# One power on GpSimd for the inverse root of the norms, and the kept first block in place of a rebuilt one

## The chip, the cores and the metric

The kernel runs on one core of a Trainium2 chip. The metric is the device time of one execution in microseconds (us), the median of three runs.

A core has a matrix engine (TensorE, PE in the profile, with PEld for its weight loads), a vector engine (VectorE, DVE), a scalar engine (ScalarE, ACT), a general engine (GpSimd, POOL), and a queue engine (SyncE, SP). Each works through its own list of instructions in order, and waits for the others through semaphores.

## The reference

Two layers of a decoder trunk, on 2048 positions of width 1024: first a gated matrix memory (mLSTM), then a gated linear recurrence (RG-LRU), each behind an RMS norm with a residual sum, and a last RMS norm. The part that the change touches is the norm, and the projection behind it:

```python
def rmsnorm(x, g):
    xf = x.astype(jnp.float32)
    y = xf * lax.rsqrt(jnp.mean(xf * xf, axis=-1, keepdims=True) + EPS)
    return (y * g.astype(jnp.float32)).astype(x.dtype)
...
    for layer in range(DEPTH):
        u = rmsnorm(x, ln_g[layer])
        if layer % N_MIXERS == 0:
            y = mlstm_mixer(u, ...)      # proj = u @ w_in, then convolution, gates, memory, w_out
        else:
            y = rglru_mixer(u, ...)      # proj = u @ w_in, then convolution, gates, scan, w_out
        x = x + y
    return rmsnorm(x, final_g)
```

## The kernel before, in words

The activations are held transposed: a tile has 128 of the 1024 features on its partitions and 512 positions (one block) along it. There are four blocks. Every float32 product is done as three matmuls of rounded parts: a number is split into `hi` and `lo` (`split_into`, lines 735 to 738: ACT makes `hi`, DVE subtracts it to make `lo`), and `mm3` (lines 362 to 364) adds hi*hi, hi*lo and lo*hi.

The phases follow one another: `phase_a1` (first norm and first projection, up to about 1000 us), `phase_a2` (the matrix memory, to about 1710 us), `phase_b1` (output projection of layer one, second norm and second projection, to about 2560 us), `phase_b2` (gates, scan, output projection, last norm).

**Slabs.** The two projections use a scheme of seven products in place of eight (Winograd's form of Strassen's) on a *slab* of two blocks. A slab `s` consists of a first block and a second one. The first block gives `u`, its normed value, in eight tiles `xs`, split into the operands `u11` (features 0 to 511) and `u21` (512 to 1023). The second block `x1` is scaled to its own `u`, and both are combined into the operands `t1` to `t4` and `u22`. `combos` (line 196) does this on DVE: it scales eight tiles (line 207) with the rows of the inverse root, and makes the sums and differences and their splits, some 44 DVE steps for a slab. While DVE does so, the PE has only products of the first block to work on: `early` (line 230) runs 6 weight groups with `u11` and `u21` alone, and calls hooks between them: `stat` (line 607) and `norm` (line 610). `stat` makes the inverse root of the second block's norm (`invrms`) and calls `backs` (line 187), which rebuilds the first block's `u` from its parts, eight DVE additions `hi + lo` (line 185) into the tiles `t1h` and `t4l`. `norm` calls `combos`. `group` (line 249) then runs the remaining five products of each weight group. The second projection (`phase_b1`) uses the same helpers.

**Norms.** `stats_sum` (line 1019) adds the squares over the partitions with 4 small matmuls (`ssum`, line 1024), forms mean + eps on DVE (`stx`, line 1027: 128 x 4 numbers), and calls `rsqrt` (line 334). This starts from the shifted bit pattern (lines 338 and 339) and makes three Newton rounds of three steps (lines 341 to 343): eleven DVE steps on 128 x 4 numbers, each needing the one before. The result `rc` is spread over the partitions by the matmuls `rows` (line 140) or `srow` (line 1034). There are twelve such norms: four blocks for each of three RMS norms.

**Weights.** Raw weights come by SP's queue into eight `raw` buffers, are combined on DVE (`sum`, line 117), split into eight slots `s`, and the splits of combined weights are stored by POOL's queue (`d_wx`, `d_wr`; line 90) for the second slab.

**Order.** The program hands the instructions to a planner, which orders them for each engine by priority and by the time at which it reckons them ready; weight preparation has high priority. So the order on an engine is not the order of the program text, and the order of one engine can put a step behind another that waits.

The matrix memory (`phase_a2`) already has a power on POOL, for its own norm of two numbers a partition (line 967).

Of the kernel before, what the change touches and what calls it, by code (L numbers as in the profile page):

```python
# [7 lines left out]
F32 = mybir.dt.float32  # L8
F32R = mybir.dt.float32r
I32 = mybir.dt.int32  # L10
AF = mybir.ActivationFunctionType
ALU = mybir.AluOpType
PSUM = bass.MemoryType.PSUM

P = 128
T = 2048
DM = 1024
KD = DM // P
# [8 lines left out]
EPS = 1e-6  # L27
# [11 lines left out]
class Slab:  # L39
# [153 lines left out]
            self.back(f2[j], U, "u21", j, self.nc.vector)  # L193
        return f1, f2

    def combos(self, U, xs, rc, fs, row=None):

        f1, f2 = fs
        v = self.nc.vector
        pb = self.rows(rc)  # L200
        if row is not None:
            self.nc.scalar.copy(row, pb)
            pb = row
        us = xs if row is not None else [self.x() for _ in range(KD)]
        for j in range(4):
            for k in (j, j + 4):
                v.scalar_tensor_tensor(us[k], xs[k], self.K.v(self.gain, k), pb, op0=ALU.mult, op1=ALU.mult)
            x12, x22 = us[j], us[j + 4]
            t = self.temp("t4", "h", j)
            v.tensor_tensor(t, x22, x12, op=ALU.subtract)  # L210
            U["t3", j] = self.operand("t3", j, t, "v")
            v.tensor_tensor(x12, x12, f1[j], op=ALU.subtract)
            v.tensor_tensor(f1[j], f1[j], t, op=ALU.add)
            U["t2", j] = self.operand("t2", j, f1[j], "v")
        for j in range(4):
            U["u22", j] = self.operand("u22", j, us[j + 4], "v")
            v.tensor_tensor(us[j + 4], f2[j], f1[j], op=ALU.subtract)
        for j in range(4):
            U["t1", j] = self.operand("t1", j, us[j], "v")
        for j in range(4):  # L220
            U["t4", j] = self.operand("t4", j, us[j + 4], "v")
# [67 lines left out]
class Trunk:  # L289
    def __init__(self, ctx, tc, vecs, gbias):  # L290
        self.tc = tc
        self.nc = nc = tc.nc
        cp = ctx.enter_context(tc.tile_pool(name="const", bufs=1))
        self.cp = cp
        self.tail = []
        self.vec = cp.tile([P, NVEC], F32, name="vec")
        nc.sync.dma_start(self.vec, vecs)
        self.gb = cp.tile([64, 2], F32, name="gb")
        nc.sync.dma_start(self.gb, gbias)
        self.ident = cp.tile([P, P], F32, name="ident")  # L300
        make_identity(nc, self.ident)
        self.ones = cp.tile([P, 1], F32, name="ones")
        nc.vector.memset(self.ones, 1.0)
        self.one1 = cp.tile([1, 1], F32, name="one1")
        nc.vector.memset(self.one1, 1.0)
        self.lc = cp.tile([P, 48], F32, name="lc")
        self.gT = cp.tile([P, 64], F32, name="gT")
        self.wlT = cp.tile([P, 64], F32, name="wlT")
        self.enT = cp.tile([P, 64], F32, name="enT")
        self.dl = cp.tile([P, 64], F32, name="dl")  # L310
# [20 lines left out]
        o = VOFF[name] + i  # L331
        return self.vec[:, o:o + 1]

    def rsqrt(self, pool, out, x, w, rows=P):
        nc = self.nc
        b = pool.tile([P, w], I32, tag="rsb", name="rsb")
        t = pool.tile([P, w], F32, tag="rst", name="rst")
        nc.vector.tensor_scalar(b[:rows], x.bitcast(I32), 1, None, op0=ALU.logical_shift_right)
        nc.vector.tensor_scalar(out.bitcast(I32), b[:rows], -1.0, float(0x5F3759DF), op0=ALU.mult, op1=ALU.add)
        for _ in range(3):  # L340
            nc.vector.tensor_tensor(t[:rows], out, out, op=ALU.mult)
            nc.vector.scalar_tensor_tensor(t[:rows], t[:rows], -0.5, x, op0=ALU.mult, op1=ALU.mult)
            nc.vector.scalar_tensor_tensor(out, t[:rows], 1.5, out, op0=ALU.add, op1=ALU.mult)

    def stats(self, pool, psp, acc, rc, rb, tag="st"):

        nc = self.nc
        ps = psp.tile([P, 512], F32, tag=tag, name=tag)
        for c in range(4):
            nc.tensor.matmul(ps[:, c:c + 1], acc[:, c * P:(c + 1) * P], self.ones, start=True, stop=True)  # L350
        x = pool.tile([P, 4], F32, tag="stx", name="stx")
        nc.vector.tensor_scalar(x, ps[:, 0:4], 1.0 / DM, EPS, op0=ALU.mult, op1=ALU.add)
        self.rsqrt(pool, rc, x, 4)
        pb = psp.tile([P, 512], F32, tag=tag, name=tag)
        for c in range(4):
            nc.tensor.matmul(pb[:, c * P:(c + 1) * P], rc[:, c:c + 1].to_broadcast([P, P]), self.ident,
                             start=True, stop=True)
        nc.scalar.copy(rb, pb)

    def mm3(self, out, sh, sl, mh, ml, first, last, resumed=False):  # L360
        mm = self.nc.tensor.matmul
# [23 lines left out]
    def phase_a1(self, xT, woq, wxz, D):  # L385
        tc, nc = self.tc, self.nc
        with ExitStack() as ctx:
            S = Slab(self, ctx, "g0")
# [93 lines left out]
            def load(b):  # L482

                xs = fetch([S.x() for _ in range(KD)], b)
                return xs, squares(xs)

            def ahead(b):
                return fetch(S.ahead(), b)
# [103 lines left out]
            with tc.high_priority():  # L592
                xs, acc = load(0)
                prefetch(1)
                x1 = ahead(1)
                acc1 = squares(x1, True)
            pb = S.rows(S.invrms(acc))
            U = {}
# [5 lines left out]
            for s in range(2):  # L604
                t = []

                def stat():
                    t[:] = [S.invrms(acc1), S.backs(U)]

                def norm():  # L610
                    S.combos(U, x1, *t)
                p1 = S.early(NE, lambda j: ew[j] if j < 2 * s else stream(1, s), U, lambda j: out_of(first[j], s),
                             ([] if s else [None, None]) + [stat, norm])
                for j, i in enumerate(first):
                    S.group(stream(), U, out_of(i, s), p1=p1[j])
                gates = iter(())
                for j, (kind, i) in enumerate(middle):
                    W = stream()
                    if kind == "q":
                        o_group(W, i, s, U)  # L620
                        if i == H - 1 and s == 1:
                            gates = self.gates(wk, pm, G, D)
                        continue
                    if s == 0 and j == 1:
                        lt = wk("lam")
                        parts = iter(range(8))

                        def lpart(r, w):
                            i = next(parts) * 64
                            return lt[0:r, i:i + w]  # L630
                        self.decay_rates(lpart)
                    next(gates, None)
                    if s == 0 and j == 5:
                        xs, acc = load(2)
                    if s or j < len(middle) - 1:
                        n2 = {}
                        if s == 0 and j == len(middle) - 3:
                            rc = []
                            n2 = {"t2": lambda: rc.append(S.invrms(acc)), "t1": lambda: S.scale(xs, rc[0])}
                        S.group(W, U, out_of(i, s), n2)  # L640
                        continue
                    V, n1 = {}, []
                    with tc.high_priority():
                        er = [S.raws(wxz[i], ("11", "12")) for i in first[0:2]]

                    def after_t2():
                        S.parts(V, xs[0:4], "u11", "v")
                        n1.extend(ahead(3))

                    def after_u21():  # L650
                        for e, r in enumerate(er):
                            ew.append({nm: S.operand("t3", e * 2 + q, r[nm], "v") for q, nm in enumerate(r)})
                        S.parts(V, xs[4:8], "u21", "v")
                    S.group(W, U, out_of(i, s), {"t2": after_t2, "u21": after_u21, "t4": lambda: n1.append(squares(n1, True))})
                    U = V
                    x1, acc1 = n1[0:KD], n1[KD]
# [362 lines left out]
    def stats_sum(self, pool, psp, sums, rc, tag):  # L1019
        nc = self.nc  # L1020
        ps = psp.tile([P, 512], F32, tag=tag, name="ssum")
        for c in range(4):
            for i, a in enumerate(sums):
                nc.tensor.matmul(ps[:, c:c + 1], a[:, c * P:(c + 1) * P], self.ones, start=i == 0,
                                 stop=i == len(sums) - 1)
        x = pool.tile([P, 4], F32, tag="stx", name="stx")
        nc.vector.tensor_scalar(x, ps[:, 0:4], 1.0 / DM, EPS, op0=ALU.mult, op1=ALU.add)
        self.rsqrt(pool, rc, x, 4)

    def stats_rows(self, psp, rc, tag):  # L1030
        nc = self.nc
# [466 lines left out]
```

## Time and profile before

| | us |
|---|---|
| median of three runs | 3058.34 (3058.22 to 3059.42) |
| profiled execution | 3061.18 |
| its span in the profile | 3059.1 |
| PE busy in the span | 2927.9 |
| DVE busy | 2153.6 |
| ACT busy | 1509.3 |
| POOL busy | 211.7 |

The granted clock of the PE over the span is 0.983 of full speed.

How to read the profile lines below. A line of a group names the source line, the engine, the operation, the tiles (out<-in), shapes and the count; behind the bar stand the busy time in us, the mean of one in ns, and the idle time of that engine just before. A line of the timeline begins with the start and the duration in us, and ends with the idle time before it and what ended that, in brackets. A line of waits has the total in us, the number of times, and the longest. A line of the windows has a stretch, its length, and the busy time of PE, PEld, DVE, ACT and POOL with the number of instructions, then the granted clock, the share of the DMA engines, and GB/s. Times count from the start of the span.

### The profile page before, as it was taken

How to read it: one execution, taken by the hardware profiler on the slowest of the kernel's cores; microseconds unless marked ns; L12 is line 12 of the kernel's file. 1: busy time of each engine (PE TensorE's matmuls, PEld its weight loads, DVE VectorE, ACT ScalarE, POOL GpSimd, SP SyncE). 2: the span in 40 equal slices, each digit the busy share in tenths (PEclk: the TensorE clock that was granted, in tenths of full speed). 3: DMA queues.
4: the chain of work that ended last, by engine and by line, in shares of the span. 5: the costliest groups of instructions: out<-in, count | busy, mean ns of one | idle time of the engine just before them, and what ended most of it. 6: DMA issues, size and time to landing. Idle time of an engine off the chain costs nothing. (4 is left out here: it accounts for less than half of the span.)

```text
span 3059.1 us, 43718 instructions
## 1 busy us (share of the span) xinstructions
PE 2927.9 (96%) x15730; PEld 2506.7 (82%) x15730; DVE 2153.6 (70%) x3774; ACT 1509.3 (49%) x2514; POOL 211.7 (7%) x394
## 2 busy tenths in 40 slices
PE   6999999999999999999999899999999998899997
PEld 4799987899988898989999777877888886687786
DVE  7866789534566688888888555687778374887775
ACT  5444545323344566666666322333445234876772
POOL 0111110000000011111111000000110000110100
PEclk9999999999999999999999999999999998999999
DMA  6766677666777645454443665566666656656643
GB/s 218 255 216 231 230 249 241 204 202 206 222 222 228 193 129 167 128 171 132 148 144 102 200 192 176 182 210 216 217 216 224 206 188 230 240 183 236 237 134 128
DMA packets 308985, 600.63 MB, mean 196 GB/s; under 512 B 27808, under 2 KB 106400, under 8 KB 308768
## 3 DMA queue, kind: packets, MB, share of 16 engines
q1 hardware_dynamic: 222784, 389.79, 41.4%
q10 hardware_dynamic: 59184, 107.77, 10.0%
q0 software_dynamic: 26800, 100.28, 8.5%
q8 instruction: 124, 2.03, 0.3%
q14 instruction: 93, 0.76, 0.1%
HBM read 388.86 MB, written 208.86 MB: 195 GB/s over the span
## 5 line engine op out<-in xcount | busy, mean ns | idle before, releaser
L735 ACT CAST s<-raw 128x512 fp32r<-128x512 f32 (+1 forms) x360 | 222.3, 621 | 497.8 <-PE acc L364 195.4
L738 DVE TENSOR_TENSOR s<-raw,s 128x512 fp32r<-128x512 f32 (+1 forms) x360 | 246.9, 689 | 90.4 <-ACT s L735 84.9
L362 PE MATMUL acc<-yh,s 128*128 128x512 f32 x512 | 202.3, 398 | 10.1 <-ACT yh L735 3.4
L363 PE MATMUL acc<-yl,s 128*128 128x512 f32 x512 | 202.8, 396 | 0.0
L364 PE MATMUL acc<-yh,s 128*128 128x512 f32 x512 | 202.2, 395 | 0.0
L362 PE MATMUL acc<-yh,wh 128*128 128x512 f32 x384 | 150.4, 399 | 14.3 <-ACT yh L735 9.4
L363 PE MATMUL acc<-yl,wh 128*128 128x512 f32 x384 | 153.5, 401 | 0.3 <-DVE yl L738 0.2
L364 PE MATMUL acc<-yh,wl 128*128 128x512 f32 x384 | 152.1, 399 | 1.1 <-DVE wl L738 1.0
L662 DVE SCALAR_TENSOR_TENSOR xc<-xm,vec,xc 128x512 f32<-128x512 f32 x192 | 140.5, 748 | 14.3 <-ACT xc L660 13.4
L735 ACT CAST s<-sum 128x512 fp32r<-128x512 f32 (+1 forms) x120 | 74.3, 620 | 146.4 <-PE pa L364 43.6
L362 PEld LDWEIGHTS acc<-yh,s 128*128 128x128 f32 x512 | 96.6, 189 | 35.5 <-ACT yh L735 3.8
L735 ACT CAST wh<-wr 128x512 fp32r<-128x512 f32 (+1 forms) x104 | 65.4, 641 | 107.8 <-PE acc L363 76.1
L364 PEld LDWEIGHTS acc<-yh,s 128*128 128x128 f32 x512 | 96.8, 189 | 22.7
L363 PEld LDWEIGHTS acc<-yl,s 128*128 128x128 f32 x512 | 96.8, 189 | 22.4 <-DVE yl L738 0.4
L930 DVE SCALAR_TENSOR_TENSOR C<-C,dl,kv 128x516 f32<-128x516 f32 x112 | 83.7, 747 | 44.6 <-PE kv L364 44.5
L738 DVE TENSOR_TENSOR wl<-wr,wh 128x512 fp32r<-128x512 f32 (+1 forms) x104 | 73.5, 717 | 56.2 <-ACT wh L735 50.9
L362 PE MATMUL gate<-xch,wh 128*128 128x512 f32 x224 | 91.9, 411 | 19.2 <-ACT xch L735 9.3
L738 DVE TENSOR_TENSOR s<-sum,s 128x512 fp32r<-128x512 f32 (+1 forms) x120 | 82.6, 689 | 39.3 <-ACT s L735 38.0
L662 DVE SCALAR_TENSOR_TENSOR xc<-xr,vec,xc 128x512 f32<-128x512 f32 x144 | 104.9, 747 | 7.3 <-ACT xc L660 6.3
L735 ACT CAST Ch<-C 128x516 fp32r<-128x516 f32 x120 | 74.8, 623 | 64.9 <-DVE da L948 48.2
L362 PE MATMUL pj<-vwh,xmh 128*128 128x512 f32 x256 | 103.3, 403 | 0.0
L364 PE MATMUL pj<-vwh,xml 128*128 128x512 f32 x256 | 100.4, 392 | 0.0
(418 smaller groups left out, 9615.2 us busy)
## 6 DMA issues: line engine op xcount, KB each, us to landing
d_wx<-s POOLq DMA_DIRECT2D x64, 512.0 KB, 4.0
s<-d_wx SPq DMA_DIRECT2D x64, 512.0 KB, 4.4
raw<-in_wout_dram SPq DMA_DIRECT2D x128, 256.0 KB, 3.1
raw<-in_wxz_dram SPq DMA_DIRECT2D x124, 256.0 KB, 4.4
d_wr<-s POOLq DMA_DIRECT2D x48, 512.0 KB, 3.5
s<-d_wr SPq DMA_DIRECT2D x48, 512.0 KB, 4.6
wr<-in_rwout_dram SPq DMA_DIRECT2D x96, 256.0 KB, 2.9
raw<-in_rwin_dram SPq DMA_DIRECT2D x84, 256.0 KB, 3.9
```

The lines of the kernel that those rows point to most:

```text
L362: mm(out, sh, mh, start=first, stop=False, skip_group_check=resumed)
L363: mm(out, sh, ml, start=False, stop=False, skip_group_check=resumed)
L364: mm(out, sl, mh, start=False, stop=last, skip_group_check=resumed)
L662: nc.vector.scalar_tensor_tensor(out, x[:, j:j + TB], self.v(wn, m * 4 + j), out, op0=ALU.mult, op1=ALU.add)
L735: a = nc.scalar.copy(hi, src)
L738: b = (nc.gpsimd if lo_eng == "p" else nc.vector).tensor_tensor(lo, src, hi.bitcast(F32), op=ALU.subtract)
L930: nc.vector.scalar_tensor_tensor(C2, C2, self.dl[:, r:r + 1], p2, op0=ALU.mult, op1=ALU.add)
```

## The change

The eleven DVE steps of `rsqrt` become one `tensor_tensor` on GpSimd with the power operation and a constant tile of -0.5, for all twelve norms. The function `stats`, which nothing called, is taken out.

In the first projection, `stat` no longer calls `backs`; it hands on the eight tiles `xs`, which hold `u` of the slab's first block since it was scaled in place. `combos` gets `held=True`: it scales the second block into the tiles `t4l` and `t1h` (where the rebuilt `u` was), and, once `u22` is split, writes its last difference over the kept tiles `xs[4:8]`. The second projection still calls `backs`.

```diff
-    def combos(self, U, xs, rc, fs, row=None):
+    def combos(self, U, xs, rc, fs, row=None, held=False):
...
-        us = xs if row is not None else [self.x() for _ in range(KD)]
+        if held:
+            us = [self.temp("t4", "l", j) for j in range(4)] + [self.temp("t1", "h", j) for j in range(4)]
+        else:
+            us = xs if row is not None else [self.x() for _ in range(KD)]
...
             U["u22", j] = self.operand("u22", j, us[j + 4], "v")
+            if held:
+                us[j + 4] = f2[j]
             v.tensor_tensor(us[j + 4], f2[j], f1[j], op=ALU.subtract)
...
+        self.mhalf = cp.tile([P, 4], F32, name="mhalf")
+        nc.vector.memset(self.mhalf, -0.5)
...
-    def rsqrt(self, pool, out, x, w, rows=P):
-        nc = self.nc
-        b = pool.tile([P, w], I32, tag="rsb", name="rsb")
-        t = pool.tile([P, w], F32, tag="rst", name="rst")
-        nc.vector.tensor_scalar(b[:rows], x.bitcast(I32), 1, None, op0=ALU.logical_shift_right)
-        nc.vector.tensor_scalar(out.bitcast(I32), b[:rows], -1.0, float(0x5F3759DF), op0=ALU.mult, op1=ALU.add)
-        for _ in range(3):
-            nc.vector.tensor_tensor(t[:rows], out, out, op=ALU.mult)
-            nc.vector.scalar_tensor_tensor(t[:rows], t[:rows], -0.5, x, op0=ALU.mult, op1=ALU.mult)
-            nc.vector.scalar_tensor_tensor(out, t[:rows], 1.5, out, op0=ALU.add, op1=ALU.mult)
+    def rsqrt(self, out, x, w):
+        self.nc.gpsimd.tensor_tensor(out, x, self.mhalf[:, 0:w], op=ALU.pow)
...
                 def stat():
-                    t[:] = [S.invrms(acc1), S.backs(U)]
+                    t[:] = [S.invrms(acc1), (xs[0:4], xs[4:8])]
 
                 def norm():
-                    S.combos(U, x1, *t)
+                    S.combos(U, x1, *t, held=True)
...
-        self.rsqrt(pool, rc, x, 4)
+        self.rsqrt(rc, x, 4)
```

More of the change, by code (lines that the diff above doesn't have):

```diff
@@ L332, in v @@
         return self.vec[:, o:o + 1]
-    def rsqrt(self, pool, out, x, w, rows=P):
-        nc = self.nc
-        b = pool.tile([P, w], I32, tag="rsb", name="rsb")
-        t = pool.tile([P, w], F32, tag="rst", name="rst")
-        nc.vector.tensor_scalar(b[:rows], x.bitcast(I32), 1, None, op0=ALU.logical_shift_right)
-        nc.vector.tensor_scalar(out.bitcast(I32), b[:rows], -1.0, float(0x5F3759DF), op0=ALU.mult, op1=ALU.add)
-        for _ in range(3):
-            nc.vector.tensor_tensor(t[:rows], out, out, op=ALU.mult)
-            nc.vector.scalar_tensor_tensor(t[:rows], t[:rows], -0.5, x, op0=ALU.mult, op1=ALU.mult)
[L343 to L352, printed above, removed]
-        self.rsqrt(pool, rc, x, 4)
[L354 to L358, printed above, removed]
+    def rsqrt(self, out, x, w):
+        self.nc.gpsimd.tensor_tensor(out, x, self.mhalf[:, 0:w], op=ALU.pow)
     def mm3(self, out, sh, sl, mh, ml, first, last, resumed=False):
@@ L1027, in stats_sum @@
         nc.vector.tensor_scalar(x, ps[:, 0:4], 1.0 / DM, EPS, op0=ALU.mult, op1=ALU.add)
-        self.rsqrt(pool, rc, x, 4)
+        self.rsqrt(rc, x, 4)
     def stats_rows(self, psp, rc, tag):
```

## The prediction

> **What bounds the kernel now.** I read the page first, then the PE's waits, then the busy times by stretch, then the instructions of the stretches that the edit touches.
>
> ```profile
> PE 2927.9 (96%) x15730; PEld 2506.7 (82%) x15730; DVE 2153.6 (70%) x3774; ACT 1509.3 (49%) x2514; POOL 211.7 (7%) x394
> PEclk9999999999999999999999999999999998999999
> ```
>
> The PE is busy for 96% of the span, nearly always at full clock, so only the 131 us in which it idles, and its slow matmuls after a pause, can be won. One pause carries the name of the edited lines (window 0 to 110 us):
>
> ```profile
> PE rows L140 <- DVE rc L343: 10.1, 2, 5.7
> ```
>
> By stretches of the first projection (columns: PE, weight loads, DVE, ACT, POOL, each with its instructions, then granted clock, DMA share, GB/s):
>
> ```profile
> 48.00:57.00 9.00, 3.34 (x15) 2.67 (x14) 6.32 (x17) 1.31 (x3) 0.53 (x1) 0.77 0.93 271
> 57.00:69.40 12.40, 12.40 (x51) 10.08 (x50) 11.38 (x19) 7.76 (x14) 1.36 (x3) 0.89 0.46 155
> 69.40:84.00 14.60, 11.22 (x31) 6.78 (x31) 14.32 (x25) 7.50 (x13) 0.77 (x2) 0.77 0.40 152
> 84.00:110.00 26.00, 26.00 (x114) 20.96 (x113) 22.35 (x37) 11.24 (x19) 4.26 (x8) 1.00 0.88 308
> ```
>
> At full clock 114 matmuls take 26.00 us, 0.23 each. The 31 of the third row are then 7.1 us of work in 14.6: 7.5 lost, while DVE is busy for 14.32 of 14.60. The PE waits there for the operands that `combos` makes on DVE, and `combos` began late because of the norms:
>
> ```profile
> 41.76 0.15 DVE L1027 TENSOR_SCALAR stx<-ssum 128x4 f32<-128x4 f32 x1
> 41.87 0.69 DVE L117 TENSOR_TENSOR sum<-sum,raw 128x512 f32<-128x512 f32 x1
> 42.48 0.69 DVE L117 TENSOR_TENSOR sum<-raw 128x512 f32<-128x512 f32 x1
> 43.09 0.17 DVE L338 TENSOR_SCALAR rsb<-stx 128x4 int32<-128x4 int32 x1
> 43.16 0.69 DVE L185 TENSOR_TENSOR temp<-u21h,u21l 128x512 f32<-128x512 f32 x1
> ...
> 52.53 0.69 DVE L117 TENSOR_TENSOR sum<-sum,raw 128x512 f32<-128x512 f32 x1 [1.01 <-DMA raw<-in_wxz_dram]
> ...
> 55.17 0.15 DVE L343 SCALAR_TENSOR_TENSOR rc<-rst,rc 128x4 f32<-128x4 f32 x1
> 57.49 2.07 DVE L207 SCALAR_TENSOR_TENSOR x<-temp,vec,rows 128x512 f32<-128x512 f32 x3 [2.17 <-PE rows L140]
> ...
> 82.14 0.69 DVE L738 TENSOR_TENSOR t2l<-temp,t2h 128x512 fp32r<-128x512 f32 x1
> ```
>
> ```profile
> 49.32 0.40 PE L364 MATMUL pa<-u21h,s 128*128 128x512 f32 x1
> 55.38 2.07 PE L140 MATMUL rows<-ident,rc 128*128 128x128 f32 x8 [5.66 <-DVE rc L343]
> ```
>
> From `stx` (41.76) to the last `rc` (55.32) the eleven small steps take 13.6 us, since each queues on DVE behind large ones; the PE stands for 5.66. Lost in all from 48 to 84: 5.7 + 1.1 (rows at half speed, 2.07 for about 0.95) + 0.7 (51 matmuls, 11.7 of work, in 12.40) + 7.5 = 15.0 us.
>
> **The change part by part.** What goes from DVE, and what comes on POOL (groups of instructions):
>
> ```profile
> L185 DVE TENSOR_TENSOR temp<-u21h,u21l 128x512 f32<-128x512 f32 x16 | 10.9, 685 | 0.0
> L341 DVE TENSOR_TENSOR rst<-rc 128x4 f32<-128x4 f32 x36 | 5.8, 160 | 0.8
> ```
> ```profile
> L967 POOL TENSOR_TENSOR frs<-frs,mh 128x2 f32<-128x2 f32 x32 | 23.3, 728 | 0.0
> L969 POOL TENSOR_TENSOR frs<-frs 128x2 f32<-128x2 f32 x32 | 6.2, 195 | 2.5
> ```
>
> Removed: 12 x 11 small DVE steps, and L185 in the two first-projection calls (8 adds each; the calls in the second projection stay). A small step followed by an independent one costs only its slot (43.09 to 43.16: 0.07), so eleven cost 0.8 us of DVE, but up to 2.2 where they stand alone; an add costs a slot of 0.6 (41.87 to 42.48), eight 4.8. Added: 12 powers of 128x4. The power of 128x2 takes 0.728, a product of that size 0.195, so the power itself is 0.53 for two columns: between 0.73 (width free) and 0.195 + 2 x 0.53 = 1.25 for four. I take 1.25, as its price over the product must lie in the elements. One memset more costs nothing (DVE idles at the start). No DMA is added or moved; on POOL the power stands among the stores of the split weights, which then wait for it, and whose slots (eight) the next splits want; that lasts as long as the power is held:
>
> ```profile
> 2745.72 1.73 DVE L738 TENSOR_TENSOR xcl<-xc,xch 128x1536 fp32r<-128x1536 f32 x1
> 2747.37 0.68 DVE L738 TENSOR_TENSOR wl<-wr,wh 128x512 fp32r<-128x512 f32 x1
> 2747.97 1.75 DVE L1321 TENSOR_TENSOR g<-xc,g 128x1536 f32<-128x1536 f32 x1
> ```
> ```profile
> 2745.93 3.84 POOL L1320 COPY hcarry<-xc 128x3 f32<-128x3 f32 x1 [23.54 <-DVE xc L1318]
> ```
>
> A POOL copy of three columns lasted 3.84 us, from 2745.93 to 2749.77, and ended as the third of three DVE ops in a row ended (2749.72). So a POOL instruction that reads SBUF can be held through a whole run of DVE ops with two SBUF inputs. This is what the power pays for leaving DVE, and the trace has no power beside such a run.
>
> *Startup.*
> ```profile
> 15.33 0.16 DVE L1027 TENSOR_SCALAR stx<-ssum 128x4 f32<-128x4 f32 x1 [1.35 <-PE ssum L1024]
> 15.41 0.69 DVE L738 TENSOR_TENSOR s<-raw,s 128x512 fp32r<-128x512 f32 x1
> ...
> 19.45 0.16 DVE L343 SCALAR_TENSOR_TENSOR rc<-rst,rc 128x4 f32<-128x4 f32 x1
> 19.64 2.29 DVE L479 TENSOR_TENSOR temp<-temp 128x512 f32<-128x512 f32 x3
> ```
> Now 15.49 to 19.61; rows, scaling and first matmul follow directly. Free of DVE: 15.6 + 1.25 = 16.9, gain 2.7. Held: three L738 close up to 17.3 and seven L479 follow, to 21.4 at slots of 0.6: `rc` at 22.6, loss 3.0. But the L479 chain adds into one tile, 2.29 us for three, 0.8 apart where ops last 0.69, so there is a gap of 0.1 behind the first one, at about 17.9: `rc` about 18.6 to 19.1. I take a gain of 1.0 (the row of the L479 decides).
>
> The Trainium skill ("SBUF — State Buffer", section "Who interferes with whom") says that a DVE instruction with two SBUF inputs blocks a GpSimd instruction that reads SBUF for that instruction, the later one to issue waiting. By that rule the power would wait for one L738 only, start at 16.1, and startup would gain 2.2 instead of 1.0; the 3.84 us row speaks for more than one, and the trace decides.
>
> *First-projection stage.* After `stx` two L117 follow (to 43.17), then a split that waits for ACT; the power gets in there, `rc` at about 44.5 instead of 55.32. Then DVE is the limit until `t2l` (82.83). It loses five of the eight adds (three stand ahead of 41.15, where it waits for a transfer), 5 x 0.6 = 3.0, small steps 0.8, and its idle 1.01 + 2.17 + some 0.8 are filled: 7.8. Less 0.8 for its own holds by the power: 7.0. Bounds: if held to the first large gap (before 52.53), `rc` comes near 52.8, gain 2.5; above, all 15.0 lost there. The next to be late is DVE again; some 8 us of PE loss stay.
>
> *Elsewhere.*
> ```profile
> 532.03 0.50 PE L362 MATMUL pd<-u22h,s 128*128 128x512 f32 x1 [0.80 <-DVE z L253]
> 1910.44 1.13 PE L140 MATMUL rows<-ident,rc 128*128 128x128 f32 x8 [1.09 <-DVE rc L343]
> 2102.55 0.79 PE L362 MATMUL pa<-u21h,s 128*128 128x512 f32 x1 [5.61 <-ACT p L263]
> ```
> At 532 the adds of the second slab stand before the awaited DVE result: 0.8 (0 to 0.8). At 1910 the wait for `rc` goes: 1.1 (0 to 1.1); DVE has free time there. ```profile
> 498.00:516.00 18.00, 13.89 (x48) 10.03 (x47) 15.48 (x31) 11.39 (x21) 0.78 (x2) 0.81 0.97 317
> ```
> At 2102 ACT waits for a DVE queue with eleven small steps in it: 0.9 (0 to 2). The norm of the third block, on DVE from 461 to 469, adds to the DVE backlog before the pause in the last row (48 matmuls, 11 us of work, in 18): likewise 0.9 (0 to 3). The six other norms (near 536, 1994 and 2114, and three in the last phase) have no PE wait behind them: 0, covered by matmuls under way; without this cover each would still cost 1.25 in place of the steps' 2.2.
>
> *End* (no cover, nothing on DVE to hold the power):
> ```profile
> 3045.78 0.16 DVE L1027 TENSOR_SCALAR stx<-ssum 128x4 f32<-128x4 f32 x1 [2.54 <-PE ssum L1024]
> ...
> 3047.96 0.16 DVE L343 SCALAR_TENSOR_TENSOR rc<-rst,rc 128x4 f32<-128x4 f32 x1
> 3048.17 1.78 PEld L1034 LDWEIGHTS srow<-ident,rc 128*128 128x128 f32 x8 [2.52 <-DVE rc L343]
> ```
> 3045.94 to 3048.12, 2.2; with 0.1 to reach POOL and 1.25: gain 0.8 (to 1.4 at 0.73).
>
> Holding `u` in its eight tiles to the end of `combos` costs nothing: the next use of those slots is a load some 400 us later. The tiles that take the scaled block are the ones `backs` wrote, so no new wait for a free one.
>
> **Sum:** 1.0 + 7.0 + 0.9 + 0.8 + 1.1 + 0.9 + 0.8 = 12.5 us. The profiled execution took 3061.18 (span 3059.1), 2.8 above the median 3058.34. From the median: **3045.8 us**.
>
> **Rivals.** *Held (faster little, or same).* The power waits out every DVE run: -3.0 + 2.5 + 4.5 for the rest = 4.0, **3054.3**. For it: the 3.84 row. Against: gaps at L479 and after the L117 pair.
>
> *Behind stores (slower).* POOL works in order; its stores in the stage wait for splits:
> ```profile
> 44.82 0.68 POOL L90 DMA_DIRECT2D d_wx<-s  x1 [43.53 <-DVE rst L341]
> ...
> 63.45 0.53 POOL L90 DMA_DIRECT2D d_wx<-s  x1 [14.32 <-DVE s L738]
> ...
> 72.17 0.53 POOL L90 DMA_DIRECT2D d_wx<-s  x1 [2.54 <-DVE s L738]
> ```
> If the order puts the power behind that of 72.17, `rc` comes at 73.95 and `t2l`, after 2.2 for rows and 20.5 of `combos` (25.3 less eight weight ops of 0.6 done earlier), at 96.6, 13.8 late; less 5.5 won elsewhere, 8.3 slower: **3066.6**. It breaks even behind 63.45 (`rc` 65.2). Against: `stx` is done at 41.91, before the first store.
>
> *More.* If the PE's loss there goes whole and the other terms reach their upper ends, 2.7 + 15.0 + 0.8 + 1.1 + 2 + 3 + 1.4 = 26: **3032**. Against: DVE's 14.32 of 14.60.
>
> **How the numbers follow.** 0.2% (6 us) is about what this kernel's timing can tell from none. Forecast (6 to 18 us won) 0.60; more 0.10; held 0.20; behind stores, or an order made worse by the same planner elsewhere, 0.10. So faster 0.70, same 0.21, slower 0.09. Range 3037 to 3056: below it about half of "more", above it "behind stores" and the worse part of "held". The likeliest alone: 3040 to 3052.
>
> **What would show it.** After: L338 to L343 gone, twelve POOL powers of 0.7 to 1.3 us, longer ones where DVE runs; 16 L185 left; the first `rows` wait at about 18 us, the second gone; first L207 near 46 instead of 57.5; the PE still pausing between 60 and 75. Wrong, if powers last over 3 us, if a POOL store stands ahead of one, if the PE's loss in the stage stays although L207 starts early, or if waits appear away from the twelve norms.

## The result and the profile after

| | before | after |
|---|---|---|
| median of the runs, us | 3058.88 (3058.22 to 3065.8) | 3045.43 (3042.1 to 3045.67) |
| ratio after to before, 95% interval | | 0.9946 (0.9933 to 0.9958) |
| profiled execution, us (span) | 3061.18 (3059.1) | 3042.1 (3040.0) |

The prediction was 3045.8 us. The change won 13.4 us in the medians, and 19.1 us between the two profiled executions; of these 19.1, 3.3 arise between 1010 and 1712 us, in the matrix memory, which the change does not touch.

From the page after, the busy times (PE, its weight loads, DVE, ACT, POOL):

```profile
PE 2922.0 (96%) x15730; PEld 2504.1 (82%) x15730; DVE 2128.0 (70%) x3627; ACT 1508.6 (50%) x2514; POOL 225.6 (7%) x406
```

DVE has 147 instructions less: 132 small steps and 16 additions went, and one memset came. POOL has the twelve powers, at 1.2 us in the mean (groups of instructions):

```profile
L343 POOL TENSOR_TENSOR rc<-stx,mhalf 128x4 f32<-128x4 f32 x12 | 14.7, 1225 | 412.5 <-DVE stx L1012 410.6 <-DVE hist L1141 1.7
```

The PE's waits from 0 to 110 us: the second wait for `rc`, 5.7 us before, is gone; the first one is left, at 1.7. The longest of the stage is now one for an operand of `combos`, 2.4:

```profile
PE pc L347 <- ACT t3h L720: 2.4, 1, 2.4
PE rows L140 <- POOL rc L343: 1.7, 1, 1.7
```

Startup and the second norm, on POOL, PE and DVE (timelines of the kernel after; start, duration):

```profile
15.97 1.41 POOL L343 TENSOR_TENSOR rc<-stx,mhalf 128x4 f32<-128x4 f32 x1 [14.67 <-DVE stx L1012]
40.12 1.39 POOL L343 TENSOR_TENSOR rc<-stx,mhalf 128x4 f32<-128x4 f32 x1 [22.74 <-DVE stx L1012]
43.39 0.74 POOL L90 DMA_DIRECT2D d_wx<-s  x1 [1.88 <-DVE s L723]
```

```profile
17.43 2.07 PE L140 MATMUL rows<-ident,rc 128*128 128x128 f32 x8 [1.74 <-POOL rc L343]
...
20.99 1.22 PE L347 MATMUL pa<-u11h,s 128*128 128x512 f32 x2 [1.49 <-ACT u11h L720]
...
44.67 1.05 PE L140 MATMUL rows<-ident,rc 128*128 128x128 f32 x8
```

```profile
15.72 0.16 DVE L1012 TENSOR_SCALAR stx<-ssum 128x4 f32<-128x4 f32 x1 [1.35 <-PE ssum L1009]
15.80 1.90 DVE L723 TENSOR_TENSOR s<-raw,s 128x512 fp32r<-128x512 f32 x3
...
47.45 0.74 DVE L211 SCALAR_TENSOR_TENSOR temp<-temp,vec,rows 128x512 f32<-128x512 f32 x1
```

The power at startup began beside a run of three DVE steps (15.80 to 17.70) and was done at 17.38, before the run was. In the second norm `rc` was ready at 41.51, but its `rows` stand behind other matmuls in the PE's order and ran at 44.67 without any wait.

The stage by stretches, with the same bounds as in the prediction (columns as there):

```profile
48.00:57.00 9.00, 9.00 (x41) 7.29 (x40) 9.00 (x16) 6.70 (x13) 0.53 (x1) 1.00 1.01 381
57.00:69.40 12.40, 9.04 (x30) 5.38 (x29) 12.40 (x21) 7.43 (x13) 1.59 (x3) 0.85 0.66 238
69.40:84.00 14.60, 14.60 (x58) 11.75 (x58) 13.35 (x23) 6.82 (x12) 1.59 (x3) 0.89 0.54 172
84.00:110.00 26.00, 25.12 (x109) 20.05 (x109) 20.63 (x33) 9.89 (x17) 4.25 (x8) 1.00 0.97 349
```

From 48 to 57 the PE goes from 3.34 us busy to 9.00. A pause of some 3.4 us and slow matmuls stay, now at 57 to 69.4.

To see where time is won, I set the k-th matmul of one trace against the k-th matmul of the trace before. "Lead" below is how much earlier it starts. Counted from 0, matmul 16 starts at 23.29 us in the kernel before (end of startup), 114 at 48.15, 274 at 100.02, and the first `srow` of the last norm at 3048.17.

### The profile page after: what moved, and what is told of

It reads as the page before. It is cut to its first block, busy times and chain, and to the rows that moved or that the text cites. A ratio compares the mean times of both kernels' runs of the same rounds, so it can differ in the third digit from the quotient of the medians.

```text
span 3040.0 us, 43598 instructions
## 1 busy us (share of the span) xinstructions
PE 2922.0 (96%) x15730; PEld 2504.1 (82%) x15730; DVE 2128.0 (70%) x3627; ACT 1508.6 (50%) x2514; POOL 225.6 (7%) x406
## 5 line engine op out<-in xcount | busy, mean ns | idle before, releaser
L347 PEld LDWEIGHTS acc<-yh,wh 128*128 128x128 f32 x384 | 72.9, 191 | 33.4 <-ACT yh L720 11.3
```

What stands on the lines that cost most here:

```text
L347: mm(out, sh, mh, start=first, stop=False, skip_group_check=resumed)
```

## The experiments

The ratios compare each kernel with the kernel before on the chip that ran both; the leads set one profile of each against the one profile of before, so a few tenths of a us between two rows say nothing (the two profiles of the change differ by 0.4 in the stage). The table collects the stage for all; "weight steps" are the DVE steps that write `sum` or `s`, counted if they begin before 66 us; "first scaling" is the first step of `combos` with the rows.

| kernel | ratio to before (95%) | lead at 16 | at 114 | at 274 | stage (114 to 274) | weight steps by 66 us | first scaling |
|---|---|---|---|---|---|---|---|
| before | 1 | 0 | 0 | 0 | 0 | 25 | 57.49 |
| after | 0.9946 (0.9933 to 0.9958) | 2.3 | 2.8 | 9.3 | +6.5 | 30 | 47.45 |
| after, again | 0.9955 (0.9942 to 0.9967) | 2.8 | 2.3 | 8.3 | +6.1 | 30 | 47.66 |
| kept tiles only | 0.9967 (0.9956 to 0.9979) | -0.5 | 0.5 | 7.0 | +6.5 | 30 | 50.06 |
| power in first two norms | 0.9965 (0.9953 to 0.9977) | 2.2 | 2.2 | 8.6 | +6.4 | 30 | 47.54 |
| four powers | 0.9994 (0.9985 to 1.0002) | -0.9 | -0.4 | 6.6 | +7.0 | 30 | 50.84 |
| after, combos later | 0.9960 (0.9946 to 0.9973) | 2.3 | 1.1 | 6.3 | +5.3 | 30 | 52.72 |
| power only, combos later | 0.9976 (0.9967 to 0.9985) | 2.4 | 1.3 | 1.4 | 0.0 | 27 | 55.71 |
| after, rows early | 0.9988 (0.9978 to 0.9998) | 2.4 | 0.5 | 0.0 | -0.5 | 23 | 43.31 |
| power only | 0.9998 (0.9989 to 1.0006) | 2.3 | 2.4 | -5.3 | -7.6 | 23 | 54.13 |
| power only, combos first | 1.0014 (1.0006 to 1.0023) | 2.6 | 0.1 | -6.8 | -6.9 | 19 | 44.51 |
| after, additions unused | 1.0009 (1.0001 to 1.0018) | 3.0 | 2.9 | -6.7 | -9.6 | 23 | 54.66 |

**The power alone**

```diff
-                    t[:] = [S.invrms(acc1), (xs[0:4], xs[4:8])]
+                    t[:] = [S.invrms(acc1), S.backs(U)]
...
-                    S.combos(U, x1, *t, held=True)
+                    S.combos(U, x1, *t)
```

> The power for all twelve norms, but the first block's u still rebuilt by the eight additions. Theory (the early start of the combos in a stage limited by DVE is most of the gain; the kept tiles only take five additions of 0.6 us out of that stage): startup 2.3 us, stage 7.1 less 3.0, the norms near 461, 1910, 2102 and at the end together about 4, so some 10 us below the kernel before: 3048.5 us (3046 to 3051). Rival A (other DVE work fills the place of the additions, the kept tiles are worth nothing): 3045.5. Rival B (the stage's gain comes from the additions that went, the power is worth startup and end alone): 3053 to 3055.

Measured: no gain at all, 0.9998. It wins its startup (2.3) and loses 7.6 in the stage. None of the three numbers expected holds, and with them falls the reading that an early `rc` is worth most of the gain. Two of the PE's waits there (timeline of the power alone):

```profile
53.67 0.80 PE L349 MATMUL pa<-u11h,s 128*128 128x512 f32 x1 [3.77 <-DVE s L723]
...
63.12 0.64 PE L347 MATMUL pb<-t2h,s 128*128 128x512 f32 x1 [1.85 <-ACT t2h L720]
```

It no longer waits for `rows` but for a weight split `s`. On DVE and ACT, same kernel:

```profile
40.42 0.68 DVE L185 TENSOR_TENSOR temp<-u11h,u11l 128x512 f32<-128x512 f32 x1
...
51.12 0.69 DVE L117 TENSOR_TENSOR sum<-sum,raw 128x512 f32<-128x512 f32 x1 [1.59 <-DMA raw<-in_wxz_dram]
51.72 0.68 DVE L185 TENSOR_TENSOR temp<-u21h,u21l 128x512 f32<-128x512 f32 x1
52.33 1.89 DVE L723 TENSOR_TENSOR s<-raw,s 128x512 fp32r<-128x512 f32 x3
54.13 2.05 DVE L211 SCALAR_TENSOR_TENSOR x<-temp,vec,rows 128x512 f32<-128x512 f32 x3
```

```profile
81.45 0.62 ACT L720 CAST s<-sum 128x512 fp32r<-128x512 f32 x1 [4.23 <-PE pb L349]
81.97 0.62 ACT L720 CAST t1h<-x 128x512 fp32r<-128x512 f32 x1
```

The additions stand among the splits and sums of the weights. Such a step that comes late leaves its `raw` buffer full, and the next load comes late: of the loads of raw weights, one is issued at 46.30 us, behind the sum of 45.59, and the next only at 53.04, behind the first split of 52.33. DVE stands 1.59 us for a load, and the split that the PE waits for is behind that. Later the ACT stands 4.23 us for a weight slot which the PE frees only at the end of `pb`, with the cast to `t1h` behind it.

**The kept tiles alone**

```diff
-    def rsqrt(self, out, x, w):
-        self.nc.gpsimd.tensor_tensor(out, x, self.mhalf[:, 0:w], op=ALU.pow)
+    def rsqrt(self, pool, out, x, w, rows=P):
...
```

> The kept tiles, but the eleven DVE steps for every norm. Theory: five additions of 0.6 us less in the stage, 3 us, and the eight additions before the wait at 532, 0.5 to 0.8 us: 3055 us (3053.5 to 3056.5). Rival A (kept tiles worth nothing): 3058.5. Rival B (the additions carry the stage): 3051 or less. A gain of this kernel and one of the power alone that add up to much less than the 13.4 us of both would say that they share one wait.

Measured: 0.9967, some 10 us. Rival B holds: the additions carry the stage. The stage's +6.5 are those of the whole change, although `rc` is made by eleven steps and the first scaling comes at 50.06. By stretches (the kept tiles alone):

```profile
48.00:57.00 9.00, 9.00 (x44) 7.27 (x43) 7.71 (x14) 5.03 (x11) 1.06 (x2) 1.00 0.78 262
57.00:69.40 12.40, 8.54 (x33) 6.09 (x33) 12.40 (x22) 7.42 (x14) 1.59 (x3) 0.96 0.80 295
```

**The power for the first two norms only**

```diff
-        self.rsqrt(rc, x, 4)
+        self.norms = getattr(self, 'norms', 0) + 1
+        if self.norms <= 2:
+            self.rsqrt(rc, x, 4)
+        else:
+            self.newton(pool, rc, x, 4)
```

> Kept tiles; the power for the first two norms only (startup and the first slab's second block), the eleven DVE steps for the other ten. Theory (the first 110 us carry the gain): startup 2.3, stage 7.1, the additions before 532 0.5, less about 1 given back by 150 us: 9 to 10 us won, 3049 us (3047.5 to 3050.5), the PE's matmuls some 9 us earlier from 100 us on and no more than 10 to the end. Rival C (the ten other norms carry half or more, since they stand before DVE backlogs): 3052 to 3054.

Measured: 0.9965, 10.7 us of 3060, and 8.6 us of lead at matmul 274. So the first 110 us do carry most of the gain, as the theory had it, though not for its reason.

**Four powers in place of one**

```diff
-        self.nc.gpsimd.tensor_tensor(out, x, self.mhalf[:, 0:w], op=ALU.pow)
+        for _ in range(4):
+            self.nc.gpsimd.tensor_tensor(out, x, self.mhalf[:, 0:w], op=ALU.pow)
```

> As the changed kernel, with the power of each norm done four times in a row into the same tile, so each chain is about 3.0 us longer (three times 1.01 us, and what DVE holds up). Theory (the power's length is on the path at startup and at the end only, and in part at 1912): startup +3.0, end +3.0, stage 0 (rc at 44.6 in place of 41.5, and its rows were not issued before 44.67), at 1912 and 2102 0 to +2 each: 3051.5 to 3055.5. Rival D (each of twelve norms pays): +36, 3081. Rival E (its length is covered nearly everywhere): 3046 to 3048.

Measured: 0.9994, so 12 to 15 us dearer than the change; more than the theory's 6 to 10, far less than 36. Startup pays 3.2 and the last norm 3.8. The stage pays nothing (+7.0), with `rc` 6.2 us (47.73) and the first scaling 3.4 us later than in the change. The excess is in the second projection: from 1800 to 2110 us the lead falls by 4.5 us. The PE's waits for the power over the whole span, first in the change, then with four powers:

```profile
PE rows L140 <- POOL rc L343: 2.8, 3, 1.7
...
PE srow L1019 <- POOL rc L343: 1.3, 1, 1.3
```

```profile
PE rows L140 <- POOL rc L344: 13.1, 3, 5.1
...
PE srow L1020 <- POOL rc L344: 4.6, 1, 4.6
```

The same three waits and the last one, each three to four us longer: at startup (5.1), at two norms of the second projection (8.0 together), and at the end. At these four of twelve norms the length of the power is on the path.

**Rows early**

```diff
-        pb = self.rows(rc)
+        if held:
+            with self.K.tc.high_priority():
+                pb = self.rows(rc)
+        else:
+            pb = self.rows(rc)
...
-                    t[:] = [S.invrms(acc1), (xs[0:4], xs[4:8])]
+                    with tc.high_priority():
+                        r1 = S.invrms(acc1)
+                    t[:] = [r1, (xs[0:4], xs[4:8])]
```

> The changed kernel, with the second block's norm and the rows that spread it at high priority in the planner, so that the rows come 18 matmuls earlier in the PE's order (rc was ready at 41.5 us, its rows ran at 44.7, the first scaling at 47.45). Theory after the runs with one part each (the stage is set by how many DVE steps stand in it, not by when rc comes): at most 1 us faster than the changed kernel, 0.9943 to 0.9950 of the kernel before. Rival (the start of the combos counts, as the prediction had it): the 3 us are won, 0.9935 or less.

Measured: 0.9988, 10 to 13 us slower than the change. Neither expected a loss. The first scaling comes at 43.31, 4 us earlier than in the change, and the stage loses all its gain: the planner puts 14 weight steps ahead of it on DVE in place of 20. The PE's longest wait in the stage is then this one (its timeline):

```profile
81.86 0.50 PE L352 MATMUL pd<-t1l,s 128*128 128x512 f32 x1 [4.45 <-DVE t1l L729]
```

**Combos first, and additions unused**

```diff
 (to the power alone)
-                        S.combos(U, x1, *t)
+                    with tc.high_priority():
+                        S.combos(U, x1, *t)
```

> As the power alone (additions kept), with all of the combos at high priority in the planner. In the power alone, the ACT's cast of a weight stood ahead of the cast to t1h and waited 4.23 us for the PE to free its slot (81.45), while the PE waited for t1. Theory (the 7.6 us that the power alone lost in the stage are this order): most of it comes back, stage shift at 100 us at least +1 us where the power alone had -5.3, and 0.9980 or less of the kernel before. Rival (the additions leave DVE no room whatever the order): 0.9990 to 1.0000, shift at 100 us below -3.

Measured: 1.0014, and -6.9 in the stage: high priority for the combos does not repair it. 19 weight steps have passed by 66 us, the fewest of all.

```diff
 (to the change)
                     t[:] = [S.invrms(acc1), (xs[0:4], xs[4:8])]
+                    S.backs(U)
```

> The changed kernel with the eight additions of both slabs done again and their result not used: the combos still take the kept tiles. Theory (eight DVE slots in the way of weight splits and combos cost the stage 7 to 8 us, more than their 4.8 us of slots): the stage's shift at 100 us falls from 9.3 to about 2, and the kernel is at 0.9968 to 0.9978 of the kernel before. Rival A (it is the combos' need of them that costs, unused ones go into gaps): 0.9945. Rival B (they cost their slots, no more): shift 4.5 to 6, 0.9960.

Measured: 1.0009, and the stage goes from +6.5 to -9.6. Eight additions whose result nobody reads, 4.8 us of slots, take 16 us there. Both rivals' numbers fall; the theory had the sign and half the size. One thing was not taken apart: the additions write the tiles `t1h` and `t4l`, into which `combos` then scales the second block, so the scalings still had to stand behind them (first at 54.66), and no run has unused additions in tiles of their own. By stretches, and DVE's timeline, first one step of the change and then three of this kernel:

```profile
48.00:57.00 9.00, 4.12 (x13) 2.98 (x12) 6.25 (x11) 1.24 (x2) 0.00 (x0) 0.76 0.53 164
```

```profile
39.95 0.68 DVE L723 TENSOR_TENSOR s<-raw,s 128x512 fp32r<-128x512 f32 x1
```

```profile
39.83 0.68 DVE L185 TENSOR_TENSOR temp<-u11h,u11l 128x512 f32<-128x512 f32 x1
...
51.64 0.69 DVE L117 TENSOR_TENSOR sum<-sum,raw 128x512 f32<-128x512 f32 x1 [2.75 <-DMA raw<-in_wxz_dram]
...
52.85 1.89 DVE L724 TENSOR_TENSOR s<-raw,s 128x512 fp32r<-128x512 f32 x3
```

The PE is back at 4.12 of 9.00 us, and DVE itself is busy for 6.25 only: it stands 2.75 us for a weight that is not loaded yet, while the DMA engines are busy for 0.53 of the stretch (1.01 in the change). In the change, DVE splits raw weights at 39.95, 41.80, 43.00 and 44.52 us; here additions stand in those places (39.83, 41.63, 42.84, 44.40), and the next split of a raw weight comes at 52.85.

> The changed kernel unaltered, to stand beside the others on the same chip. Every theory expects the ratio of its first runs, 0.9933 to 0.9958, and a stage shift of 9 to 10 us at 100 us. What differs between this profile and the first one in the matrix memory (1400 to 1710 us), which the change does not touch, is the scatter between executions: 0 to 5 us.

Measured: 0.9955, with 16.9 us of lead in this profile.

**Combos one weight group later**, with and without the additions

```diff
-                             ([] if s else [None, None]) + [stat, norm])
+                             [stat, norm] if s else [None, None, stat, None, norm])
```

> The power alone (additions kept), with the combos of the first slab called one weight group later. In the DVE's order 30 weight steps then stand ahead of the last scalings, as in the kernel before, where the power alone had 23. Theory (the order, not the power or the additions by themselves, cost the power alone its 7.6 us between 48 and 100 us): the shift against the kernel before between 48 and 100 us lies at -1 to +4, and the kernel at 0.9965 to 0.9985. Rival (eight additions in the stage cost 7 to 10 us with any order): -5 or worse, 0.9990 to 1.0005.

> The changed kernel with the combos of the first slab called one weight group later. In the DVE's order 23 weight steps (combinations and splits) then stand ahead of the first scaling in place of 20, and 30 ahead of the fourth. Theory after the last four runs (the stage goes well where 30 weight steps pass DVE before the last scalings, and badly where 23 do; when the combos begin is of little account): within 3 us of the changed kernel, 0.9940 to 0.9962 of the kernel before. Rival (the earlier the combos, the better): later combos lose 2 to 4 us more, 0.9965 to 0.9975.

Measured: the power alone recovers from 0.9998 to 0.9976, and its stage from -7.6 to 0.0, by this one move; in the DVE's order 30 weight steps stand ahead of its last scalings, where the power alone had 23. The change itself is not better for it (0.9960; stage +5.3). The theory holds in both. The two kernels differ by the additions (and the tiles that go with them), and by 5.3 us in the stage: about their 4.8 us of slots. So of the 14.1 us that divide the change from the power alone in the stage (+6.5 to -7.6), some 7.6 are the order of the power alone, 5.3 the additions themselves, and 1.2 what the change loses with later combos. No kernel run here beat the change.

**What POOL waits for beside DVE**

```python
for w, two in ((0, 0), (512, 1), (1536, 1), (512, 0), (1536, 0)):
    for kind in ("pow", "mul", "copy", "carry"):
...
            nc.vector.tensor_scalar(big[:, 0:4], last, 0.25, 1.0, op0=ALU.mult, op1=ALU.add)
            for q in range(4 if w else 0):
                if two:
                    nc.vector.tensor_tensor(r[q][:, 0:w], big[:, 0:w], c[:, 0:w], op=ALU.mult)
...
            if kind == "pow":
                nc.gpsimd.tensor_tensor(o, big[:, 0:4], mh, op=ALU.pow)
...
```

> Nothing of the reference is computed; the outputs get a constant. A DVE step of 128x4 releases one POOL instruction and, right behind it on DVE, four independent steps of 512 or 1536 columns, with two SBUF inputs or with one. The POOL instruction is a power of 128x4, a product of 128x4, a copy of 128x4, or a copy of three columns 512 apart as in the last phase. Theory (POOL waits for the one DVE step it meets): power 1.0 alone, 1.4 beside 512 columns, 2.6 beside 1536; the copies 0.4 to 0.6 and 1.7. Rival (a copy waits through the whole run, as the 3.84 us row read, and the power does not): copy of three columns about 2.4 us beside four steps of 512 columns and 6.5 beside four of 1536. Rival (all kinds wait through a run of such steps where nothing else comes between): power 3.4 and 7.5. With one-input steps no waiting in any case.

Measured, in groups ("0a" alone, "b" beside two-input steps, "a" beside one-input steps of that width):

```profile
L1475 POOL TENSOR_TENSOR pow1536b<-big,mh 128x4 f32<-128x4 f32 x3 | 7.7, 2579 | 11.1 <-DVE big L1468 11.1
L1475 POOL TENSOR_TENSOR pow1536a<-big,mh 128x4 f32<-128x4 f32 x3 | 5.5, 1822 | 5.4 <-DVE big L1468 5.4
L1482 POOL COPY carry1536b<-big 128x3 f32<-128x3 f32 x3 | 5.3, 1778 | 15.9 <-DVE big L1468 15.9
...
L1475 POOL TENSOR_TENSOR pow512b<-big,mh 128x4 f32<-128x4 f32 x3 | 4.5, 1512 | 2.9 <-DVE big L1468 2.9
...
L1475 POOL TENSOR_TENSOR pow0a<-big,mh 128x4 f32<-128x4 f32 x3 | 3.0, 1011 | 4.5 <-DVE big L1468 4.5
```

One step and no more, for the copy too (1.78, where four steps last 6.76). One-input steps hold it as well, for their shorter time, which no theory expected. The last run varied when POOL arrives:

> Nothing of the reference is computed; the outputs get a constant. A run of DVE steps with two SBUF inputs (five of 512 columns, or 1536, 512 and 1536 as in the last phase) stands on DVE, and an ACT copy of 8 to 1024 columns, started with the run, releases a POOL instruction that so arrives 0.2 to 1.5 us into it: a power of 128x4, or the copy of three strided columns. In the first probe all arrived 0.05 us after a step had begun and waited for that one step. Theory (one step always): whenever it arrives, the copy ends with the step that it met, the power 0.8 us after that step. Rival (who arrives later than some 0.15 us into a step is kept back by the next one too, to the end of the run, as the 3.84 us row read): late copies end at the end of the run, at about 3.1 us for five steps of 512 columns and 4.0 for the mixed run, and late powers 0.8 after.

```profile
156.82 4.03 DVE L1475 TENSOR_TENSOR r<-big,c 128x1536 f32<-128x1536 f32 x3
157.92 0.70 POOL L1479 COPY carry_three_n<-mid 128x3 f32<-128x3 f32 x1 [3.64 <-ACT mid L1473]
```

In all 40 cases the POOL instruction waits for the one step that it met: the 20 copies end 0.04 to 0.06 us behind the end of that step, the 20 powers 0.86 to 0.87 behind it. The rival falls. Why the copies of the last phase last longer stays open: they still do in the kernel after,

```profile
L1305 POOL COPY hcarry<-xc 128x3 f32<-128x3 f32 x16 | 40.3, 2520 | 333.6 <-DVE xc L1303 333.6
```

and one thing that the two probes left out is that DVE there reads the same tile as the copy. Of these 16 copies, six meet the step `g<-xc,g`, which reads that tile, and end with it; the other ten meet another step first and last through it and through `g<-xc,g` behind it. No run tells whether the tile is the reason.

## Why the prediction came out

The time was hit within 0.4 us, but of its largest term only the size was right, and that the sum came out is in part luck: startup won some 1.5 us more than was taken, two terms can't be told from scatter or from other causes, and more than half of the stage's 7.0 was counted on an earlier `rc` and its small steps, which proved to be worth nothing there. By its steps (each with the term taken and its range):

- **Startup**, 1.0 (-3.0 to 2.7): measured 2.3 and 2.8, and 2.2 to 3.0 in every kernel with one power there; the kept tiles alone have -0.5. The step of the prediction that failed is the hold, read from one row of another kind of instruction (3.84 us). The power waited for the first of three steps and took 1.41, `rc` at 17.38 where 18.6 to 19.1 was said. The rule of the Trainium skill ("SBUF — State Buffer", "Who interferes with whom"), that a contender is blocked for one instruction, would have given 2.2; the probes agree with it (1.51 beside 512 columns, 2.58 beside 1536).
- **Stage**, 7.0 (2.5 to 15.0): measured 6.5 and 6.1. The cause was wrong. The prediction took 3.0 for the additions and got the rest from the earlier `rc`, small steps and filled idle time. The kept tiles alone give 6.5; the power adds nothing to them, and without them it costs 7.6; four powers, `rc` 6.2 us later, leave +7.0. Scaling near 46 was said: it came at 47.45, since `rows` stood 3.2 us behind `rc` in the PE's order and two weight steps were ahead of it on DVE, and it did not matter. The sum also took off 0.8 for the power's holding up DVE, a price that no row showed; in the probe DVE's steps keep their pace beside a power.

  What the sum left out is the other work on DVE: the weights. In every kernel with 30 weight steps begun by 66 us the stage wins 5.3 to 7.0; with 25 to 27 it is at 0; with 19 to 23 it is at -0.5 to -9.6. The pair that differs only in where the combos are called, and the pair that differs only in the unused additions, show that order and additions set this; that the count is the whole of it is not shown (-0.5 and -9.6 both have 23). The loads sort the profiles in the same way: by 50 us, 23 loads of raw weights have been issued in each of the six whose stage wins, and 18 to 21 in the other six. That fits the chain of late weight steps and late loads, but does not prove it.
- **Third block's norm** (461 to 469), 0.9: the lead grows by 0.9 and 2.4 from 500 to 516, but also by 1.1 and 2.4 in the two kernels with eleven steps there. It is not shown to be the power's.
- **532**, 0.8: the lead grows by 0.5 between 516 and 540 in both profiles of the change, and by 0.5 to 0.9 in the five others with kept tiles and no additions; by 0.0 in the four with the additions. The mechanism holds; the size was off by 0.3.
- **1910 and 2102**, 1.1 and 0.9: 0.4 and 0.4, then 2.1 and 0.9 in the two profiles of the change, against -0.4 and 0.2 at 1910, and -0.5 and 0.1 at 2102, in the kernels with eleven steps. Between 1800 and 2110 the lead moves by +3.5 in one profile of the change and by -1.3 in the other, so the term at 2102 isn't measured better than by 2 us. That the power wins something at both places is seen in all eight profiles with one power there: 0.4 to 0.5 at 1910, 0.7 to 2.4 at 2102.
- **End**, 0.8: 1.1 in all eight profiles with one power there. The power takes 1.01 us free, and 1.25 was taken (0.73 to 1.25).

Rivals: *held* falls, since the power waits for one step. *Behind stores* did not come, the first store stands at 43.39, 1.9 us behind the power. But its kind, an order on one engine that costs more than the edit wins, is what the power alone ran into, and the prediction gave that 0.10 on grounds that had nothing to do with the additions. *More* did not come.

## What to carry to other kernels

In a stage where one engine serves two customers (here DVE, for weights and for the combined operands), ask what each step stands in front of before asking how early the step itself can run: making one chain ready earlier let the planner put it ahead of the weights and cost 7 to 8 us in the stage, while eight steps of 0.6 us taken out were worth 1.1 to 3.4 times their slots, by the order that the rest fell into. When an edit has two parts, run each alone even where the sum comes out: here the parts gave 10 and 0, and the term that looked like the power's belonged to the additions. And price a new instruction's hold by a row of its own kind, or keep it as a bound.

## What was not expected of the hardware

A power of 128x4 on POOL takes 1.01 us alone, a product of that size 0.20, a copy 0.19. Beside steps with two inputs each ends a fixed time behind the one step that it met (0.04 to 0.06 for the copy, 0.86 to 0.87 for the power), so part of a power, some 0.15 us by these numbers, runs while it waits. One-input DVE steps hold POOL too: a copy takes 0.44 beside 512 columns and 0.98 beside 1536, where two-input steps make it 0.71 and 1.78. DVE was not slowed by it: four steps of 1536 columns took 6.76 us with the power beside them and with the copy, one every 1.67 us, also where POOL had long been done.
